# Turning the on-chip memory layout of a one-layer decoder kernel upside down

## The chip, the cores and the metric

The kernel runs on one core of a Trainium2 chip. The metric is device time in microseconds (us) of one execution of the whole program, from a launch to its end; several runs of one program are compared by their median. A profiled execution gives the start and length of every instruction as well.

SBUF is the core's on-chip memory: 128 partitions, each with its own byte addresses. [...] PSUM is the small memory that TensorE (PE) writes its products to. In one matmul the *stationary* operand (here 128x128, brought in by a weight load, PEld) stays in the array, and the *moving* operand (here mostly 128x512) streams through it. VectorE (DVE), ScalarE (ACT) and GpSimd (POOL) do the rest, and SyncE (SP) issues the DMAs.

## The reference

One decoder layer on x of 1024 tokens by 1024 channels, all float32 (cut to what is computed here):

```
def reference(x, ...):
    h = rms_norm(x, norm_mix_g)
    x = x + pool_mixer(h, pool_w, pool_b, pool_scale)   # causal windows 2, 4, 8, 16, then a 256x256 product per group
    f = conv_ffn(rms_norm(x, norm_ffn_g), w_in, conv_w, conv_b, w_out)
    return x + f

def conv_ffn(x, w_in, conv_w, conv_b, w_out):
    h = causal_depthwise_conv(x @ w_in, conv_w, conv_b)   # 1024 -> 2 * 2816, three taps
    val, gate = jnp.split(h, 2, axis=-1)
    return (jax.nn.silu(gate) * val) @ w_out              # 2816 -> 1024
```

## The kernel before

The work has three stages.

**The mixer** (to about 92 us) goes over eight tiles of 128 tokens. Its two products, `psd` (windows, line 152) and `psy` (pool weights, line 206), and the transposing product `pst` (line 229) run on PE. It leaves the second norm's output as operands of the first large product.

**The first product** (x @ w_in) goes over 22 pairs of hidden blocks `n`. Each pair is done as seven half-size products (Strassen-Winograd) instead of eight, the entries `P1` to `P7` of the table `STEPS`:

```
"P1": ("A11", "B11", "X"), "P6": ("S2", "T2", "Y"), "P5": ("S1", "T1", "Z"), "P2": ("A12", "B21", "X"),
"P7": ("S3", "T3", "Y"), "P3": ("S4", "B22", "Z"), "P4": ("A22", "T4", "Y"),
```

The first name is the stationary operand (from the weights), the second the moving one (from the activations), the third the PSUM bank. Every float32 operand is split into a high and a low half, and a step is twelve matmuls of 128x512 (function `product`, line 295): for each of four k, high x high, high x low, low x high. In the profile the moving tiles' numbers are cut off, so that a step is known by its stationary tile: `X<-B,A11s` is P1 (moving B11), `Y<-T,S2s` P6 (T2), `Z<-T,S1s` P5 (T1), `X<-B,A12s` P2 (B21), `Y<-T,S3s` P7 (T3), `Z<-B,S4s` P3 (B22), `Y<-T,A22s` P4 (T4). From n = 2 on the steps run in the order of the table.

**The second product** (gated hidden units @ w_out, line 567) is done in the same way, seven times eleven blocks of twelve matmuls, `oP<-oBP,oAP`. Both operands, moving (`oB..`) and stationary (`oA..`), are split tiles made just before use.

What matters here is where tiles lie. Tiles come from pools. A pool opened plainly is put at the lowest free address, one opened with `side="right"` at the highest:

- `nop_a` (left side): moving tiles B11, T1 and B21 of the first product, 16 KB each, from address 17,312 to 66,464.
- `work` (left side): above it. It holds `raw` (weights as loaded, 76,704 to 93,088) and `hl` (seven split tiles of 4 KB, 93,088 to 121,760). The stationary operands of the first product and both operands of the second are `hl` tiles, made by `split` (lines 69 and 70).
- `n2_pool`, later `late`, later `fin` (left side): above `work`.
- `pre` (right side): all of the mixer's own tiles, from 159,456 up. When the mixer is done, `nop_b` takes its place, with the moving tiles B22, T4, T3 and T2 at 163,808, 180,192, 196,576 and 212,960, and `right` with a small tile.

In the second product, `take` (blocks `blk`) reuses the room of `raw` and of the moving tiles.

Of the kernel before, what the change touches and what calls it, by code (L numbers as in the profile page):

```python
# [14 lines left out]
P = 128  # L15
# [8 lines left out]
WINDOWS = (2, 4, 8, 16)  # L24
HALO = 16
EPS = 1e-6
# Columns of the packed per-partition parameters: conv taps, conv bias, gains of the norms.
CW, CB, GM = 0, 3 * 2 * NF, 4 * 2 * NF
GF = GM + NK
NPAR = GF + NK  # L30
# Columns of the packed constants: identity, factors of the first rows, windows of the first tile.
FAC = P
B0 = FAC + 2 * NG * HALO
BD = B0 + NG * P
# Operands of the first product that are ready before the mixer ends; columns of the second norm's gain that ScalarE applies.
NOPS_A = 3
ACT_GAIN = 7

# [5 lines left out]
def trunk_kernel(ctx: ExitStack, tc: tile.TileContext, x, consts, par, rows, pool_w, w_in, w_out, out):  # L44
# [2 lines left out]
    const = ctx.enter_context(tc.tile_pool(name="const", bufs=1))  # L47
    dram = ctx.enter_context(tc.tile_pool(name="dram", bufs=1, space=bass.MemoryType.DRAM))
    ps_x = ctx.enter_context(tc.tile_pool(name="ps_x", bufs=2, space=PSUM))
    nop_a = ctx.enter_context(tc.tile_pool(name="nop_a", bufs=1))  # L50
    work = ctx.enter_context(tc.tile_pool(name="work", bufs=1))
    mid = ExitStack()
    n2_pool = mid.enter_context(tc.tile_pool(name="n2_pool", bufs=1))
    pre = ExitStack()
    pp = pre.enter_context(tc.tile_pool(name="pre", bufs=1, side="right"))
    ps_p = pre.enter_context(tc.tile_pool(name="ps_p", bufs=3, space=PSUM))

    def bank2(name):
# [2 lines left out]
    def raw_tile(name):  # L61
        return work.tile([P, 2, D], F32, tag="raw", name=name, bufs=2)
# [7 lines left out]
        nc.vector.tensor_tensor(t[:, 1, :], src, t[:, 0, :].bitcast(F32), ALU.subtract)  # L70
        return t

# [1 line left out]
    xs = {}  # L74

    def load_x(j):
# [10 lines left out]
    def affine(t, src, op, fill, base, pattern, step):  # L87
        nc.gpsimd.affine_select(out=t, in_=src, compare_op=op, fill=fill, base=base, pattern=pattern, channel_multiplier=step)

    nc.gpsimd.memset(x_edge[:HALO, :], 0.0)  # L90
    for g, w in enumerate(WINDOWS):
        # Row (j, r) is x[128 j - 16 + r], column (j', t) is token 128 j' + t: 1 / w where j == j' and r - 16 > t - w
        e = edge_band[:, g, :].rearrange("p (j t) -> p j t", t=HALO)
        nc.gpsimd.memset(edge_band[:, g, :], 1.0 / w)
        affine(e, e, ALU.is_gt, 0.0, w - HALO, [[-HALO, NS], [-1, HALO]], 1)
        affine(e, e, ALU.is_ge, 0.0, HALO - 1, [[HALO, NS], [0, HALO]], -1)
    for g, w in enumerate(WINDOWS):
        # 1 / w where s - w < s' <= s, less 1 where s' == s
        m = band[:, g, :]
        nc.gpsimd.memset(m, 1.0 / w)  # L100
        affine(m, m, ALU.is_ge, 0.0, 0, [[1, P]], -1)
        affine(m, m, ALU.is_gt, 0.0, w, [[-1, P]], 1)
        affine(m, m, ALU.not_equal, 1.0 / w - 1.0, 0, [[1, P]], -1)
# [24 lines left out]
    def rstd_of(src, name):  # L128
        junk = pp.tile([P, D], BF16, tag="junk", name=f"junk_{name}")
        st = pp.tile([P, 4], F32, tag="st", name=f"st_{name}", bufs=8)  # L130
        nc.scalar.activation(junk, src, AF.Square, accum_out=st[:, 0:1])
        nc.scalar.activation(st[:, 1:2], st[:, 0:1], AF.Sqrt, bias=eps_t, scale=1.0 / D)
        nc.vector.tensor_scalar(st[:, 0:1], st[:, 0:1], 1.0 / D, EPS, op0=ALU.mult, op1=ALU.add)
        nc.vector.reciprocal(st[:, 2:3], st[:, 1:2])
        # One Newton step on 1 / sqrt
        nc.vector.scalar_tensor_tensor(st[:, 3:4], st[:, 2:3], st[:, 0:1], st[:, 2:3], op0=ALU.mult, op1=ALU.mult)  # L136
        nc.vector.tensor_scalar(st[:, 3:4], st[:, 3:4], -0.5, 1.5, op0=ALU.mult, op1=ALU.add)
        nc.vector.tensor_tensor(st[:, 2:3], st[:, 2:3], st[:, 3:4], ALU.mult)
        return st[:, 2:3]
# [3 lines left out]
    def edge_norm():  # L143
        nc.vector.tensor_scalar(edge_band, edge_band, rstd_of(x_edge, "e"), None, op0=ALU.mult)
# [13 lines left out]
        windows(ps, x_edge, edge_band)  # L158
        nc.scalar.activation(edges, ps.rearrange("p (c s) -> p c s", c=NK), AF.Copy)

# [1 line left out]
    wph = pp.tile([P, 2 * NG, GRP], F32R, tag="wph", name="wph")  # L162
    wpl = pp.tile([P, 2 * NG, GRP], F32R, tag="wpl", name="wpl")

# [32 lines left out]
    def mixer_out(j):  # L197
        dh, dl = ds.pop(j)
        ps = bank2(f"psy{j}")
        for g in range(NG):  # L200
            o = ps[:, g * GRP : (g + 1) * GRP]
            n = 0
            for k in range(2):
                c = 2 * g + k
                for a, w in ((dh, wph), (dh, wpl), (dl, wph)):
                    nc.tensor.matmul(o, a[:, c, :], w[:, c, :], start=n == 0, stop=n == 5)  # L206
                    n += 1
        x1 = xs.pop(j)
        marks[j] = nc.vector.tensor_tensor(x1, ps, x1, ALU.add).ins  # L209
        nc.sync.dma_start(x1_dram[j * P : (j + 1) * P, :], x1)  # L210
        r = rstd_of(x1, f"b{j}")
        diag = pp.tile([P, P], F32, tag="diag", name=f"diag{j}", bufs=2)
        nc.vector.tensor_scalar(diag, ident, r, None, op0=ALU.mult)
        n2s[j] = (x1, diag)
# [36 lines left out]
        nc.scalar.activation(h, src, AF.Copy)  # L251
        nc.vector.tensor_tensor(t[:, 1, ks, cols], src, h.bitcast(F32), ALU.subtract)  # L252

# [1 line left out]
    order = [j + k * NP2 for j in range(NP2) for k in range(2)]  # L255
    raws, sums, aops = {}, {}, {}

# [7 lines left out]
    def add(out, a, b):  # L265
        nc.vector.tensor_tensor(out, a, b, ALU.add)
# [35 lines left out]
    banks, hid = {}, {}  # L302
# [69 lines left out]
        if p == "P4":  # L372
            gated(n)

# [1 line left out]
    def stat(j):  # L376
        if j in xs and j not in stats:
            stats[j] = rstd_of(xs[j], f"a{j}")
# [24 lines left out]
        stat(j + 2)  # L403
        stat(j + 1)
    pre.close()
    nop_b = ctx.enter_context(tc.tile_pool(name="nop_b", bufs=1, side="right"))
    right = ctx.enter_context(tc.tile_pool(name="right", bufs=1, side="right"))
    ps_yz = ctx.enter_context(tc.tile_pool(name="ps_yz", bufs=3, space=PSUM))
    for b in ("T2", "T3", "B22", "T4"):
        nops[b] = nop_tile(nop_b, b)  # L410
# [5 lines left out]
    halves = [slice(0, 2), slice(2, 4)]  # L416
# [16 lines left out]
        split_n(nops["T4"], t4[:, ks], ks=ks)  # L433
    mid.close()
    late_stack = ExitStack()
    late = late_stack.enter_context(tc.tile_pool(name="late", bufs=1))
    for k in range(9, len(events)):
        event(k)
    late_stack.close()

# [1 line left out]
    fin = ctx.enter_context(tc.tile_pool(name="fin", bufs=1))  # L442
    free = []

    def take(name):
        """Room for [P, 512] of float32, where the first product's operands were."""
        if not free:
            take.n += 1
            if take.n <= 2:
                t = raw_tile(f"blk{take.n}").rearrange("p a (b s) -> p (a b) s", s=NH)  # L450
            elif take.n <= 9:
                pool = nop_a if take.n in (3, 5, 6) else nop_b
                t = pool.tile([P, 8, NH], F32, tag="nop", name=f"blk{take.n}", bufs=NOPS_A if pool is nop_a else 7 - NOPS_A)
            else:
                return work.tile([P, NH], F32, tag="q1", name=f"blk_{name}", bufs=2)
            free.extend(t[:, i, :] for i in range(t.shape[1]))
        return free.pop(0)
# [12 lines left out]
    def load_block(name, f):  # L470
        t = blk[name, f] = take(f"{name}_{f}")
        nc.sync.dma_start(t, src[name](f))
# [38 lines left out]
    def z_tile(name, i):  # L511
        return fin.tile([P, NH], F32, tag="z", name=f"{name}_{i}", bufs=12)
# [1 line left out]
    starts = []  # L514

    def z_start(name, i, rows_, cols):
        """x1's block plus the first product."""
        z = zs[name, i] = z_tile(name, i)
        r = rows_ * NH + i * P
        nc.sync.dma_start(z, x1_dram[r : r + P, s_half[cols]])  # L520
        add(z, z, zs["q1", i])
# [15 lines left out]
    for k in range(-SLOOK, len(oevents)):  # L537
# [14 lines left out]
        if f == 0 and opens:  # L552
            for i in range(4):
                tag = ("XXYY" if set_ == "X" else "YZZZ")[i]
                pool = ps_x if tag == "X" else ps_yz
                obanks[set_, i] = pool.tile([P, NH], F32, tag=tag, name=f"o{p}{i}")
        # The last blocks of the last product go bank by bank, so that all banks but one leave early
        if k >= len(oevents) - TAIL:
            if f < NP2 - 1:
                continue  # L560
# [3 lines left out]
        for i, g in steps:  # L564
            a, b = oops[p, g]
            for m, (u, v) in enumerate(((0, 0), (0, 1), (1, 0))):
                nc.tensor.matmul(  # L567
                    obanks[set_, i], a[:, u, i * P : (i + 1) * P], b[:, v, :],
                    start=opens and g == 0 and m == 0, stop=g == NP2 - 1 and m == 2, skip_group_check=not opens,
# [24 lines left out]


def constants():
    """What the windows' shapes alone decide."""
    import numpy as np

    r, t, h = np.arange(P)[:, None], np.arange(P), np.arange(HALO)  # L600
    blocks = [np.eye(P)]
    blocks += [np.tile(w / np.minimum(h + 1, w), (P, 2)) for w in WINDOWS]
    inside = [(r > t - w) & (r <= t) for w in WINDOWS]
    blocks += [(m - np.eye(P) * np.minimum(t + 1, w)) / w for m, w in zip(inside, WINDOWS)]
    return np.concatenate(blocks, axis=1).astype(np.float32)
# [34 lines left out]
```

## Time and profile before

| | before |
|---|---|
| median of 3 runs | 739.74 us |
| the runs | 738.17, 739.74, 740.25 us |
| profiled execution: span from first to last instruction | 736.8 us |
| PE busy in that span | 700.1 us (95%) |
| DVE busy | 627.6 us (85%) |
| ACT busy | 352.3 us (48%) |
| DMA | 83.83 MB |

The page of the profile gives no total time of the profiled execution beside its span. The median of the runs is 2.9 us above the span; that is what lies around the first and the last instruction.

In rows of the timeline the columns are: start in us, length in us, engine, line of the kernel, operation, what it writes `<-` what it reads, shapes and how many instructions were merged into the row. Matmuls are pipelined: the length of one is longer than the distance to the next, so the pace of PE is read from the starts. `PEclk` is the granted TensorE clock as a share of full speed.

### The profile page before, as it was taken

To read this page: it belongs to the slowest core of one execution; us is meant where nothing else is said; L and a number is where in the kernel's file an instruction comes from. 1 tells how busy PE (TensorE), PEld (TensorE's weight loads), DVE (VectorE), ACT (ScalarE), POOL (GpSimd) and SP (SyncE) were. 2 spreads that over 40 slices of the span, in tenths; PEclk is the share of its full clock that TensorE was granted. 3 is DMA by queue.
4 is the path that set the end of the run, shared out by engine and by line. 5 is a ranking of instruction groups with operands and counts; after the bars stand their busy time and mean duration, and the time that the engine had idled before them with its cause. 6 is when DMAs were issued, how large, how long until landed. Compare 5 with 4: busy or idle time off the path is not lost.

```text
span 736.8 us, 8791 instructions
## 1 busy us (share of the span) xinstructions
PE 700.1 (95%) x3236; PEld 579.9 (79%) x3236; DVE 627.6 (85%) x928; ACT 352.3 (48%) x565; POOL 48.0 (7%) x52
## 2 busy tenths in 40 slices
PE   4688869999999999999999999999999999999997
PEld 3688857888888888888888888888887788888886
DVE  3899999999988888888888888877996898698993
ACT  5478654645444444444444444444543344444441
POOL 4523360000000000000000000000000000000000
PEclk9899989999999999999999999999999999999999
DMA  9531103133222222112122222226988920005341
GB/s 280 199 144 57 59 0 115 35 133 119 86 82 67 80 86 81 67 67 80 79 86 86 86 85 87 86 85 210 329 298 291 321 93 1 0 1 171 101 157 57
DMA packets 30882, 83.83 MB, mean 114 GB/s; under 512 B 3335, under 2 KB 4487, under 8 KB 28023
## 3 DMA queue, kind: packets, MB, share of 16 engines
q1 hardware_dynamic: 30839, 83.28, 32.3%
q8 instruction: 25, 0.41, 0.2%
q14 instruction: 18, 0.15, 0.1%
HBM read 63.34 MB, written 19.92 MB: 113 GB/s over the span
## 4 chain that ended last, share of the span: by engine, by line
PE 73%; DVE 14%; DMA 8%; issue 2%; ACT 2%; SPq 1%; DVEq 0%; ACTq 0%
PE Y L295 23%; PE oP L567 21%; PE Z L295 14%; PE X L295 14%; DMA blk<-g_dram 3%; DMA blk<-in_w_out_dram 2%; DMA x<-in_x_dram 1%; DVE T L252 1%; DVE wp_raw L168 1%; PE psy L206 1%; DMA B21s<-in_w_out_dram 1%; DVE x L209 1%; DVE dl L191 1%; DMA A12s<-g_dram 1%; DVE st_b L136 1%
## 5 line engine op out<-in xcount | busy, mean ns | idle before, releaser
L567 PE MATMUL oP<-oBP,oAP 128*128 128x512 f32 x924 | 211.3, 390 | 2.6 <-DVE oBP L70 1.7
L567 PEld LDWEIGHTS oP<-oBP,oAP 128*128 128x128 f32 x924 | 173.1, 188 | 40.6 <-DVE oBP L70 3.1
L295 PE MATMUL Z<-T,S1s 128*128 128x512 f32 x264 | 66.7, 403 | 4.4 <-DVE T L252 3.0
L295 PE MATMUL Z<-B,S4s 128*128 128x512 f32 x264 | 64.1, 392 | 1.5 <-ACT S3s L69 1.5
L295 PE MATMUL Y<-T,S3s 128*128 128x512 f32 x264 | 64.5, 393 | 0.6 <-DVE q L324 0.6
L295 PE MATMUL X<-B,A11s 128*128 128x512 f32 x264 | 64.6, 393 | 0.0
L295 PE MATMUL Y<-T,S2s 128*128 128x512 f32 x264 | 64.3, 392 | 0.0
L295 PEld LDWEIGHTS Z<-T,S1s 128*128 128x128 f32 x264 | 51.0, 194 | 16.9 <-DVE T L252 3.3
L295 PE MATMUL Y<-T,A22s 128*128 128x512 f32 x264 | 64.0, 391 | 0.0
L295 PE MATMUL X<-B,A12s 128*128 128x512 f32 x264 | 63.4, 389 | 0.0
L295 PEld LDWEIGHTS Z<-B,S4s 128*128 128x128 f32 x264 | 49.4, 188 | 12.9 <-ACT S3s L69 1.9
L295 PEld LDWEIGHTS Y<-T,S3s 128*128 128x128 f32 x264 | 49.5, 188 | 12.1 <-DVE q L324 1.0
L295 PEld LDWEIGHTS Y<-T,S2s 128*128 128x128 f32 x264 | 49.6, 188 | 11.2
L295 PEld LDWEIGHTS X<-B,A11s 128*128 128x128 f32 x264 | 49.4, 188 | 11.2
L295 PEld LDWEIGHTS Y<-T,A22s 128*128 128x128 f32 x264 | 49.6, 188 | 10.8
L295 PEld LDWEIGHTS X<-B,A12s 128*128 128x128 f32 x264 | 49.5, 188 | 10.3
L69 ACT ACTIVATE oBP<-blk 128x512 fp32r<-128x512 f32 x32 | 20.2, 633 | 46.9 <-PE oP L567 41.6
L353 ACT ACTIVATE gate<-gate 128x1024 f32<-128x1024 f32 x22 | 23.4, 1062 | 39.6 <-DVE gate L344 39.6
L343 DVE SCALAR_TENSOR_TENSOR val<-ha,par_sb,val 128x1023 f32<-128x1023 f32 x22 | 28.2, 1283 | 12.7 <-ACT val L342 12.7
L335 DVE TENSOR_TENSOR ha<-Z,q 128x512 f32<-128x512 f32 x20 | 13.8, 691 | 24.7 <-PE Z L295 24.7
L342 ACT ACTIVATE gate<-hb,par_sb 128x1024 f32<-128x1024 f32 x22 | 27.4, 1246 | 14.5 <-DVE hb L337 14.4
L342 ACT ACTIVATE val<-ha,par_sb 128x1024 f32<-128x1024 f32 x22 | 27.4, 1244 | 13.4 <-DVE ha L335 4.2
(128 smaller groups left out, 1130.2 us busy)
## 6 DMA issues: line engine op xcount, KB each, us to landing
win<-in_w_in_dram SPq DMA_DIRECT2D x22, 1024.0 KB, 4.8
g_dram<-val SPq DMA_DIRECT2D x22, 512.0 KB, 2.6
blk<-g_dram SPq DMA_DIRECT2D x33, 256.0 KB, 5.4
blk<-in_w_out_dram SPq DMA_DIRECT2D x31, 256.0 KB, 5.5
A12s<-g_dram SPq DMA_DIRECT2D x22, 256.0 KB, 4.5
B21s<-in_w_out_dram SPq DMA_DIRECT2D x22, 256.0 KB, 3.4
x<-in_x_dram SPq DMA_DIRECT2D x8, 512.0 KB, 10.5
x_dram<-x SPq DMA_DIRECT2D x8, 512.0 KB, 2.8
```

What stands on the lines that cost most here:

```text
L69: nc.scalar.activation(t[:, 0, :], src, AF.Copy)
L136: nc.vector.scalar_tensor_tensor(st[:, 3:4], st[:, 2:3], st[:, 0:1], st[:, 2:3], op0=ALU.mult, op1=ALU.mult)
L168: nc.vector.scalar_tensor_tensor(wp_raw[:, c, :], scale_b[:, g * GRP : (g + 1) * GRP], par_sb[:, GM + c : GM + c + 1], wp_raw[:, c, :], op ...
L191: nc.vector.tensor_tensor(dl, ps3, dh.bitcast(F32), ALU.subtract)
L206: nc.tensor.matmul(o, a[:, c, :], w[:, c, :], start=n == 0, stop=n == 5)
L209: marks[j] = nc.vector.tensor_tensor(x1, ps, x1, ALU.add).ins
L295: nc.tensor.matmul(bank, a[:, i, ks], b[:, l, k, :], start=opens and m == 0, stop=m == 11, skip_group_check=not opens)
L335: tt(hid[n, "a"][:, NH:], bank, hid[n, "q2"], ALU.add)
L342: nc.scalar.activation(t, src, AF.Identity, bias=par_sb[:, CB + f : CB + f + 1], scale=w[2])
L343: nc.vector.scalar_tensor_tensor(t[:, 1:], src[:, : S - 1], w[1], t[:, 1:], op0=ALU.mult, op1=ALU.add)
L353: nc.scalar.activation(gate, gate, AF.Silu)
L567: nc.tensor.matmul(obanks[set_, i], a[:, u, i * P : (i + 1) * P], b[:, v, :], start=opens and g == 0 and m == 0, stop=g == NP2 - 1 and m = ...
```

## The change

Pools are opened on the opposite side. `work`, `n2_pool`, `late` and `fin` go to the right side (the top), and `pre`, `nop_b` and `right` to the left (the bottom). `const` and `nop_a` stay. Comments and docstrings are dropped, and one blank line is added near the top, so that the lines of the kernel after stand one further down (295 becomes 296).

```diff
     nop_a = ctx.enter_context(tc.tile_pool(name="nop_a", bufs=1))
-    work = ctx.enter_context(tc.tile_pool(name="work", bufs=1))
+    work = ctx.enter_context(tc.tile_pool(name="work", bufs=1, side="right"))
     mid = ExitStack()
-    n2_pool = mid.enter_context(tc.tile_pool(name="n2_pool", bufs=1))
+    n2_pool = mid.enter_context(tc.tile_pool(name="n2_pool", bufs=1, side="right"))
     pre = ExitStack()
-    pp = pre.enter_context(tc.tile_pool(name="pre", bufs=1, side="right"))
+    pp = pre.enter_context(tc.tile_pool(name="pre", bufs=1))
...
-    nop_b = ctx.enter_context(tc.tile_pool(name="nop_b", bufs=1, side="right"))
-    right = ctx.enter_context(tc.tile_pool(name="right", bufs=1, side="right"))
+    nop_b = ctx.enter_context(tc.tile_pool(name="nop_b", bufs=1))
+    right = ctx.enter_context(tc.tile_pool(name="right", bufs=1))
...
-    late = late_stack.enter_context(tc.tile_pool(name="late", bufs=1))
+    late = late_stack.enter_context(tc.tile_pool(name="late", bufs=1, side="right"))
...
-    fin = ctx.enter_context(tc.tile_pool(name="fin", bufs=1))
+    fin = ctx.enter_context(tc.tile_pool(name="fin", bufs=1, side="right"))
```

The two built programs have the same instructions in the same order on every engine and the same semaphore waits with the same values. They differ in the SBUF addresses of tiles alone:

| tiles | address before | address after |
|---|---|---|
| moving, first product: B11, T1, B21 | 17,312 to 66,464 | the same |
| moving, first product: B22, T4, T3, T2 | 163,808 to 229,344 | 66,464 to 132,000 |
| `hl`: stationary of the first product, both operands of the second | 93,088 to 121,760 | 196,576 to 225,248 |
| `raw`: weights as loaded | 76,704 to 93,088 | 180,192 to 196,576 |
| the mixer's pool weights `wph`, `wpl` (moving) and `dh`, `dl` (stationary) | 193,248 to 209,632 and 216,032 to 228,320 | 100,256 to 116,640 and 123,040 to 135,328 |

## The prediction

> **What bounds the kernel now.** I read the page first: busy times, the clock, and the chain of work that ended last.
>
> ```profile
> span 736.8 us, 8791 instructions
> PE 700.1 (95%) x3236; PEld 579.9 (79%) x3236; DVE 627.6 (85%) x928; ACT 352.3 (48%) x565; POOL 48.0 (7%) x52
> PEclk9899989999999999999999999999999999999999
> PE 73%; DVE 14%; DMA 8%; issue 2%; ACT 2%; SPq 1%; DVEq 0%; ACTq 0%
> ```
>
> PE is busy 95% of the span and carries 73% of the chain, and after the mixer its clock is full: whatever changes the pace of a matmul changes the time. Busy time by stretch (us of the stretch, then busy us and instructions of PE, PEld, DVE, ACT and POOL, clock, DMA share, GB/s) says where:
>
> ```profile
> 119.00:519.00 400.00, 399.44 (x1741) 326.47 (x1740) 341.94 (x442) 187.57 (x252) 0.00 (x0) 1.00 0.25 92
> 525.00:737.00 212.00, 205.35 (x899) 168.02 (x897) 177.63 (x287) 87.78 (x150) 0.00 (x0) 1.00 0.43 141
> 306.95:326.23 19.28, 19.28 (x85) 15.77 (x84) 16.28 (x22) 8.96 (x12) 0.00 (x0) 1.00 0.23 82
> ```
>
> From 119 to 519 us, the first product, PE hardly stops (0.56 us in 400), while DVE has 58 us to spare. The third row is one pair n: PE without a gap, DVE 16.28 of 19.28 us. The second product waits 6.65 us in 212.
>
> The change moves no instruction and no wait; it moves addresses. So the question is whether an address shows in the pace of anything. The timeline of PE for that pair n, one row a step of twelve matmuls:
>
> ```profile
> 306.95 2.93 PE L295 MATMUL X<-B,A11s 128*128 128x512 f32 x12
> 309.72 2.93 PE L295 MATMUL Y<-T,S2s 128*128 128x512 f32 x12
> 312.48 2.93 PE L295 MATMUL Z<-T,S1s 128*128 128x512 f32 x12
> 315.25 2.88 PE L295 MATMUL X<-B,A12s 128*128 128x512 f32 x12
> 317.97 2.93 PE L295 MATMUL Y<-T,S3s 128*128 128x512 f32 x12
> 320.74 2.91 PE L295 MATMUL Z<-B,S4s 128*128 128x512 f32 x12
> 323.48 2.91 PE L295 MATMUL Y<-T,A22s 128*128 128x512 f32 x12
> 326.23 2.93 PE L295 MATMUL X<-B,A11s 128*128 128x512 f32 x12
> ```
>
> The distance from one start to the next is the cost of a step: P1 2.77, P6 2.76, P5 2.77, P2 2.72, P7 2.77, P3 2.74, P4 2.75 us, in all 19.28. Equal work, no gap, full clock, and yet nearly 2% between them. It is not the bank: P1 and P2 both write X. It isn't what runs beside them either, since the same figures come back at the first pairs, where DVE and ACT do other work:
>
> ```profile
> 138.96 2.93 PE L295 MATMUL Z<-T,S1s 128*128 128x512 f32 x12
> 141.73 2.88 PE L295 MATMUL X<-B,A12s 128*128 128x512 f32 x12
> 144.45 2.93 PE L295 MATMUL Y<-T,S3s 128*128 128x512 f32 x12
> 147.22 2.91 PE L295 MATMUL Z<-B,S4s 128*128 128x512 f32 x12
> 149.96 2.91 PE L295 MATMUL Y<-T,A22s 128*128 128x512 f32 x12
> 152.71 2.93 PE L295 MATMUL X<-B,A11s 128*128 128x512 f32 x12
> ```
>
> (2.77, 2.72, 2.77, 2.74, 2.75 again.) It fits with where the moving tile lies. P3, P4, P6 and P7 stream from `nop_b`, above 163,808, with the stationary tiles at 93,088 to 121,760: slow, 2.74 or 2.75 in the steps that follow another such step, 2.76 or 2.77 in those that come after a step from `nop_a`. P2, P1 and P5 stream from `nop_a`, below 66,464. P2, which follows another of its kind (P5), is the fast one, 2.72. P1 and P5 follow slow ones and pay 0.05 for the way back, as if two streams had to fall into step again. The spread inside the groups agrees (operation, count, then minimum, median and maximum ns):
>
> ```profile
> L295 PE MATMUL X<-B,A11s x264: 387/393/473, 74.6 to 502.3; 128*128 128x512 f32 x132
> L295 PE MATMUL X<-B,A12s x264: 387/389/476, 90.7 to 510.5; 128*128 128x512 f32 x132
> L295 PE MATMUL Z<-B,S4s x264: 388/392/503, 110.4 to 516.1; 128*128 128x512 f32 x132
> L295 PE MATMUL Y<-T,A22s x264: 388/392/394, 125.2 to 518.8; 128*128 128x512 f32 x132
> ```
>
> **What is known of other pairs of places.**
>
> ```profile
> 599.71 25.55 PE L567 MATMUL oP<-oBP,oAP 128*128 128x512 f32 x112
> 77.47 0.28 PE L206 MATMUL psy<-wph,dh 128*128 128x256 f32 x1
> 80.22 0.28 PE L206 MATMUL psy<-wph,dl 128*128 128x256 f32 x1
> ```
>
> Second product, both operands in `hl`: 112 matmuls in 25.55 us, the last of them 0.39 long as in the group's mean, so (25.55 - 0.39) / 111 = 0.2267 us each, 2.72 for twelve: the fast form. Mixer, both operands at the top (`wph` from 193,248, `dh` and `dl` from 216,032), columns 256: 24 matmuls whose first and last starts are 2.75 apart, 0.1196 each and even. So an operand high up is not slow by itself; the pair decides.
>
> **The parts of the change.**
>
> *First product.* After it all seven moving tiles lie at 17,312 to 132,000 and all stationary ones at 196,576 to 225,248. No row shows a moving tile far below its stationary one by that much; the nearest is P2 (moving at 50,080, stationary at 93,088): 2.72. All the slow rows have the moving tile above. By the sign alone all seven steps become like P2, and the two returns fall away as well: 7 x 2.72 = 19.04 against 19.28, -0.24 a pair. Pairs of the clean order run from 152.71 to 521 us, 19 of them: -4.6. Of the steps ahead of them, the five shown from 138.96 to 152.71 take 13.75 against 5 x 2.72 = 13.60, 0.15 over; the seven or so from 119 us on, at the same rate, 0.2. Together -0.4; sum -5.0. The other end for the same unknown: all seven stay at the dearest step, 2.77, or 19.39 a pair: 19 x 0.11 = 2.1, and 12 early steps x 0.02 = 0.2: +2.3. In between lies the steady slow form (2.74 and 2.75, 19.22): -0.06 x 19 = -1.1. I take -5.0, the value of the nearest row by order of the two places.
>
> *Second product.* Both operands move together from 93,088 to 196,576; their distances to each other stay. The nearest rows are itself and `psy`, both even and fast: 0. If the height of the moving tile did count for 512 columns, 77 times twelve matmuls go from 2.72 to 2.75: +2.3.
>
> *Mixer.* `psy` moves as a whole from top to bottom; 0. Its PE has gaps anyway.
>
> *DVE and ACT.* Blocks `blk` lie in `nop_b`, `nop_a` and `raw`, so at both ends, some of them 64 bytes off:
>
> ```profile
> L70 DVE TENSOR_TENSOR oAP<-blk,oAP x44: 674/683/694, 504.0 to 723.2; 128x512 fp32r<-128x512 f32 x44
> L69 ACT ACTIVATE oAP<-blk x44: 614/616/635, 503.2 to 722.4; 128x512 fp32r<-128x512 f32 x44
> ```
>
> At most 20 ns of spread in 44 places: no address price, 0. They also have slack (DVE 16.28 of what would be 19.04), so PE's gain isn't taken back by them.
>
> *DMA and what is late next.* The loads of the second product wait for the first product's moving tiles to be free, and between 513 and 560 us the chain runs over them:
>
> ```profile
> 513.56 5.52 DMA blk<-in_w_out_dram
> 530.35 6.17 DMA blk<-in_w_out_dram
> 699.84 33.11 PE oP L567 x145
> ```
>
> They start when the last steps end, so they start earlier by as much; the gain passes through. From 699.84 to the end the chain is PE's own. Same tiles and sizes: 0.
>
> **Sum.** -5.0 us on the profiled span: 736.8 to 731.8. The median lies 2.9 above the span (739.74), so 734.7. What a measurement of this kernel can tell from no change is about 0.3%, 2.2 us.
>
> **Rivals.**
>
> *A. The offset decides, not the order.* Another reading fits all the rows above as well. Distance from moving to stationary start: `nop_a` to `hl` 75,776 = 148 x 512, nothing left over; `hl` to `hl` multiples of 4,096; `wph` to `dh` 22,784, a multiple of 256. Only `nop_b` to `hl`, 70,720 = 138 x 512 + 64, is off, by 64 bytes. The right side ends where its tiles end, not on the left side's grid. After the change `hl` sits on the right side's grid and every moving tile on the left's: 179,264 = 350 x 512 + 64. Then all seven steps are in the steady slow form, without returns: -1.1, or 738.6. For it: two streams that must fall into step after each switch look like a clash by low address bits. Against it: the 64 bytes now lie on the other side.
>
> *B. The height of the moving tile decides.* First product -5.0, second +2.3: -2.7, 737.0. Against it: `psy`'s even 0.1196.
>
> *C. Slower: the search for step never ends.* If the order low under high is the worse one, what P1 and P5 pay on their way back (2.77) becomes every step's price: +2.3, 742.0. It turns slower once the mean step is above 19.28 / 7 = 2.754. For it: 2.77 is paid just by low moving tiles, with nothing left to account for. Against it: P2 settles.
>
> *D. Nothing.* 739.7, if what separates P2 from the rest is its place in the order and not its tile. Against it: P5, after P6, moves like P1, after P4, and at 138.96 to 152.71 the neighbours are others.
>
> [...]
>
> **Chances.** Forecast 0.42, A 0.33, B 0.08, C 0.12, D 0.05. The forecast's own range is 733.5 to 736. The range over the cases reaches from a full gain to D with the runs' spread, and leaves out most of C: 733.2 to 741. Faster by over 0.3%: the forecast and half of B, 0.46; within 0.3%: A, D, half of B, 0.42; slower: C, 0.12.
>
> **What would show it.** Right: in PE's timeline all seven steps 2.72 apart and a pair 19.04; medians of 389 ns in every group; the second product still 0.2267. A: all steps 2.74 or 2.75, P2 too. B: second product at 2.75 for twelve. C: steps of 2.77 and P2 among them. The forecast is wrong if P2's row, which doesn't move itself, gets slower when its stationary tile does.

## The result, and the profile after

The kernel after takes 744.9 us (median of 6 runs, 743.9 to 747.41), the kernel before 739.2 us in the same comparison (6 runs, 737.96 to 740.25): ratio 1.0094, 95% interval 1.0077 to 1.0112. It is slower by 0.9%. Forecast were 734.7 us and a range from 733.2 to 741.0.

The page after, the lines that answer to those of before:

```profile
span 743.2 us, 8791 instructions
PE 707.3 (95%) x3236; PEld 580.7 (78%) x3236; DVE 628.6 (85%) x928; ACT 352.3 (47%) x565; POOL 48.0 (6%) x52
PEclk9899989999999999999999999999999999999999
PE 80%; DVE 11%; DMA 4%; ACT 2%; issue 2%; SPq 0%; DVEq 0%; ACTq 0%
```

The long stretch of the first product by busy time (columns as in the prediction):

```profile
119.00:519.00 400.00, 399.55 (x1713) 321.61 (x1712) 340.24 (x437) 185.53 (x250) 0.00 (x0) 1.00 0.23 86
```

The same instructions, the same granted clock (1.00 from 119 to 519 us), PE 7.2 us longer busy, weight load (PEld), DVE and ACT within 1 us of before. In the 400 us of the last row PE is as full as before, but has 1713 matmuls where it had 1741. So each takes longer. The timeline of PE for one pair n:

```profile
310.85 2.96 PE L296 MATMUL X<-B,A11s 128*128 128x512 f32 x12
313.65 2.96 PE L296 MATMUL Y<-T,S2s 128*128 128x512 f32 x12
316.45 2.96 PE L296 MATMUL Z<-T,S1s 128*128 128x512 f32 x12
319.25 2.96 PE L296 MATMUL X<-B,A12s 128*128 128x512 f32 x12
322.05 2.96 PE L296 MATMUL Y<-T,S3s 128*128 128x512 f32 x12
324.85 2.96 PE L296 MATMUL Z<-B,S4s 128*128 128x512 f32 x12
327.65 2.96 PE L296 MATMUL Y<-T,A22s 128*128 128x512 f32 x12
330.45 2.96 PE L296 MATMUL X<-B,A11s 128*128 128x512 f32 x12
```

Every step starts 2.80 us after the one before: a pair is 19.60 against 19.28. No step differs from the next, and P2 (`X<-B,A12s`), whose moving tile B21 did not move, went from 2.72 to 2.80. Nineteen such pairs cost 19 x 0.32 = 6.1 us. The first product ends 7.4 us later (526.45 against 519.03): besides those 6.1, its first matmul already starts 0.8 later (75.39 against 74.62), and the steps ahead of the nineteen pairs add 0.6. The second product, from its first matmul's start to its last's, takes 1.1 us less (212.4 against 213.5), because it waits less between its steps (1.6 us idle before its matmuls against 2.6); so the span grows by 6.4 (all rounded). Weight load and matmul of P1 and P2 side by side (minimum, median and maximum ns):

```profile
L296 PEld LDWEIGHTS X<-B,A11s x264: 187/188/192, 75.4 to 509.2; 128*128 128x128 f32 x132
L296 PE MATMUL X<-B,A11s x264: 392/397/482, 75.4 to 509.4; 128*128 128x512 f32 x132
L296 PE MATMUL X<-B,A12s x264: 393/398/478, 91.4 to 517.8; 128*128 128x512 f32 x132
```

The matmul of P2 was 389 and is 398; a weight load is 188 ns. The second product kept its pace:

```profile
593.81 36.43 PE L568 MATMUL oP<-oBP,oAP 128*128 128x512 f32 x160
```

(36.43 - 0.39) / 159 = 0.2267 us each, as before.

### The profile page after: what moved, and what is told of

It reads as the page before. It is cut to its first block, busy times and chain, and to the rows that moved or that the text cites. A ratio compares the mean times of both kernels' runs of the same rounds, so it can differ in the third digit from the quotient of the medians.

```text
span 743.2 us, 8791 instructions
## 1 busy us (share of the span) xinstructions
PE 707.3 (95%) x3236; PEld 580.7 (78%) x3236; DVE 628.6 (85%) x928; ACT 352.3 (47%) x565; POOL 48.0 (6%) x52
## 4 chain that ended last, share of the span: by engine, by line
PE 80%; DVE 11%; DMA 4%; ACT 2%; issue 2%; SPq 0%; DVEq 0%; ACTq 0%
PE Y L296 24%; PE oP L568 24%; PE Z L296 15%; PE X L296 15%; DMA x<-in_x_dram 1%; DMA B21s<-in_w_out_dram 1%; DVE T L253 1%; DVE wp_raw L169 1%; PE psy L207 1%; DMA blk<-g_dram 1%; DVE x L210 1%; DVE dl L192 1%; DVE st_b L137 1%; DMA A12s<-g_dram 1%; DVE st_a L139 1%
## 5 line engine op out<-in xcount | busy, mean ns | idle before, releaser
L296 PE MATMUL X<-B,A12s 128*128 128x512 f32 x264 | 65.1, 396 | 0.0
L322 ACT ACTIVATE ha<-X 128x512 f32<-128x512 f32 x22 | 13.1, 596 | 44.3 <-PE X L296 40.7
```

The source lines that it names most:

```text
L296: nc.tensor.matmul(bank, a[:, i, ks], b[:, l, k, :], start=opens and m == 0, stop=m == 11, skip_group_check=not opens)
L322: nc.scalar.activation(hid[n, "a"][:, :NH], bank, AF.Copy)
```

## The experiments

Two theories were set against each other. **L**: what counts is the distance from the start of the stationary tile up to that of the moving one, by its low bits (rival A of the prediction, and a possible sign). **O**: what counts is which of the two lies higher, or at which end (the forecast and rival C). The kernel after, in these terms: distance from stationary up to moving, in bytes within a partition, 17,312 - 196,576 = -179,264 = -351 x 512 + 448. "Remainder" below is what such a distance leaves by 512, here 448. The remainders follow from the addresses in the built programs.

**e1, 64 unused bytes at the top** (of the kernel after, in place of the added blank line; the instructions keep their order):

```diff
+    pad = ctx.enter_context(tc.tile_pool(name="pad", bufs=1, side="right")).tile([P, 16], F32, tag="pad", name="pad")
     nop_a = ctx.enter_context(tc.tile_pool(name="nop_a", bufs=1))
     work = ctx.enter_context(tc.tile_pool(name="work", bufs=1, side="right"))
```

> The kernel after with 64 unused bytes at the very top, so that everything on the right side lies 64 bytes lower and the distance from every moving tile of the first product to the hl tiles is a multiple of 512. Theory L (the low bits of the distance between moving and stationary start decide): all seven steps of a pair take 2.72 us, P2 too, a pair 19.04; against 2.80 after, that is 7 x 0.08 x 22 = 12.3 us off, about 733 us, and some 5 us under the kernel before. Theory O (the order of the two places decides, low under high is slow): nothing changes, 2.80 a step, 744.9.

Measured 733.06 us against 738.45 for the kernel before, ratio 0.9936 (0.9912 to 0.996). PE's timeline:

```profile
312.73 2.88 PE L296 MATMUL X<-B,A12s 128*128 128x512 f32 x12
315.45 2.88 PE L296 MATMUL Y<-T,S3s 128*128 128x512 f32 x12
318.17 2.88 PE L296 MATMUL Z<-B,S4s 128*128 128x512 f32 x12
320.89 2.88 PE L296 MATMUL Y<-T,A22s 128*128 128x512 f32 x12
```

2.72 a step, all of them. Sixty-four idle bytes are worth 0.08 us a step, with the moving tiles still low and the stationary ones high. O falls, and with it the sense in which I had read the profile.

**e2, the same 64 bytes at the top of the kernel before.** Its moving tiles B22, T4, T3 and T2 stay high, 64 bytes lower.

```diff
-    nop_a = ctx.enter_context(tc.tile_pool(name="nop_a", bufs=1))
+    nop_a = ctx.enter_context(tc.tile_pool(name="nop_a", bufs=1));pad = ctx.enter_context(tc.tile_pool(name="pad", bufs=1, side="right")).tile([P, 16], F32, tag="pad", name="pad")
     work = ctx.enter_context(tc.tile_pool(name="work", bufs=1))
```

> The kernel before with 64 unused bytes at the very top, so that the right side's moving tiles (B22, T4, T3, T2) lie 64 bytes lower, a multiple of 512 from the hl tiles; they stay above the stationary tiles. Theory L: all seven steps 2.72, a pair 19.04 instead of 19.28, -5 us, about 734.5. Theory O: steps as before, 2.74 to 2.77, time as before.

Measured 733.94 us, ratio 0.9939 (0.9917 to 0.9961):

```profile
311.81 2.88 PE L295 MATMUL Z<-T,S1s 128*128 128x512 f32 x12
314.53 2.88 PE L295 MATMUL X<-B,A12s 128*128 128x512 f32 x12
317.25 2.88 PE L295 MATMUL Y<-T,S3s 128*128 128x512 f32 x12
```

2.72 again, without turning anything round. e1 and e2 are both 0.6% faster than the kernel before, and their intervals overlap.

**e3, 64 bytes low in the kernel before**, between the low moving tiles and `hl` (the edit of e2 without `side="right"`):

> The kernel before with 64 unused bytes between the low moving tiles and the work pool: hl lies 64 bytes higher, so that B11, T1 and B21 stand 64 bytes short of a multiple of 512 from it and the four tiles at the top stand right. Theory L: the roles are swapped: P3 and P4 come down to 2.72, P2 rises to 2.80 (as after), P1 and P5 near 2.80, returns at P6 and P7. Theory O: steps as before, P2 2.72, P3 2.74, P4 2.75.

Measured: 738.18 us (one run).

```profile
308.51 2.96 PE L295 MATMUL X<-B,A11s 128*128 128x512 f32 x12
311.31 2.90 PE L295 MATMUL Y<-T,S2s 128*128 128x512 f32 x12
314.05 2.96 PE L295 MATMUL Z<-T,S1s 128*128 128x512 f32 x12
316.85 2.96 PE L295 MATMUL X<-B,A12s 128*128 128x512 f32 x12
319.65 2.90 PE L295 MATMUL Y<-T,S3s 128*128 128x512 f32 x12
322.39 2.88 PE L295 MATMUL Z<-B,S4s 128*128 128x512 f32 x12
325.11 2.88 PE L295 MATMUL Y<-T,A22s 128*128 128x512 f32 x12
327.83 2.96 PE L295 MATMUL X<-B,A11s 128*128 128x512 f32 x12
```

The roles are swapped as L says: P1, P5 and P2 with the low tiles 2.80 (remainder 448, as in the kernel after), P3 and P4 with the high ones 2.72, and P6 and P7, which come after a slow step, 2.74. The high place was never the matter.

**e4, 128 bytes at the top of the kernel after**: remainder 64, the one that the high tiles had before.

> The kernel after with 128 unused bytes at the top: moving tiles still below the stationary ones, but now 64 bytes past a multiple of 512 instead of 64 short of it. Theory L with a sign: the steady slow form of before, 2.74 or 2.75 for all seven steps, a pair 19.22. L without a sign (modulus of 128): 2.80 as after. Theory O: 2.80 as after.

Measured: 736.94 us (one run).

```profile
308.15 2.91 PE L296 MATMUL X<-B,A11s 128*128 128x512 f32 x12
310.90 2.91 PE L296 MATMUL Y<-T,S2s 128*128 128x512 f32 x12
313.65 2.91 PE L296 MATMUL Z<-T,S1s 128*128 128x512 f32 x12
316.39 2.91 PE L296 MATMUL X<-B,A12s 128*128 128x512 f32 x12
```

2.75, 2.75, 2.74: exactly the steady form of before, though the order of the two places is the opposite. So 64 past a multiple costs 0.027 a step and 64 short of it 0.08. This is the kernel that rival A had in mind.

**e5 to e8, other paddings at the top of the kernel after** (192, 320, 448 and 96 bytes in place of 64):

> As the 64-byte pad, with 192 unused bytes: moving start minus stationary start leaves 128 by 512. Theory L1 (the pattern repeats every 128 bytes or less, with a sign inside): 2.72 a step. Theory L2 (it repeats every 256): neither 2.72 nor known; half a turn away, so something between 2.72 and 2.80 or more. Theory L3 (every 512): likewise unknown. Anything but 2.72 excludes L1.

> 320 unused bytes: remainder 256. L1 and L2: 2.72 a step, about 733. L3: not 2.72. The mixer's psy product, even at a remainder of 256 with 256 columns, speaks for 2.72.

> 448 unused bytes: remainder 384. L1: 2.72. L2: the same as with remainder 128. L3: another value than with 128 and 256.

> 96 unused bytes: remainder 32. If the price grows from 0 at 0 bytes to 0.027 us a step at 64, it is about 2.73 here; if places are told apart only by blocks of 64 bytes, it is 2.72 or 2.747; more than 2.75 means that the price doesn't grow with distance at all.

Measured: 746.04, 733.31, 742.76 and 746.51 us (one run each). Two starts of each, in that order:

```profile
310.36 2.96 PE L296 MATMUL X<-B,A11s 128*128 128x512 f32 x12
313.16 2.96 PE L296 MATMUL Y<-T,S2s 128*128 128x512 f32 x12
```

```profile
310.99 2.88 PE L296 MATMUL Z<-T,S1s 128*128 128x512 f32 x12
313.71 2.88 PE L296 MATMUL X<-B,A12s 128*128 128x512 f32 x12
```

```profile
309.25 2.95 PE L296 MATMUL X<-B,A11s 128*128 128x512 f32 x12
312.04 2.95 PE L296 MATMUL Y<-T,S2s 128*128 128x512 f32 x12
```

```profile
312.30 2.96 PE L296 MATMUL X<-B,A11s 128*128 128x512 f32 x12
315.10 2.96 PE L296 MATMUL Y<-T,S2s 128*128 128x512 f32 x12
```

Remainder 128 costs 2.80, so the pattern does not repeat every 128 bytes (L1 falls). Remainder 256 is free, 2.72. Remainder 384 gives 2.78 to 2.80 from step to step. Remainder 32 costs 2.80, more than 64 does: the price doesn't grow with distance, and the first two cases of the expectation, 2.73 and 2.72 or 2.747, are out.

**e9, 64 bytes at the bottom of the kernel after**, so that the moving tiles move and the stationary ones don't (the line of e1 without `side="right"`):

> The kernel after with 64 unused bytes at the bottom, ahead of the moving tiles, and nothing at the top: now the moving tiles move up by 64 and the stationary ones stay where the kernel after has them. Theory L (only the distance counts): 2.72 a step as with the 64 bytes at the top, about 733. If the absolute place of the stationary tiles in the grid counted, it stays at 2.80, about 745.

Measured: 734.69 us (one run).

```profile
311.45 2.88 PE L296 MATMUL Z<-T,S1s 128*128 128x512 f32 x12
314.17 2.88 PE L296 MATMUL X<-B,A12s 128*128 128x512 f32 x12
```

The step is 2.72: it is the same whichever of the two tiles is shifted.

**e10, `hl` tiles 4,160 bytes apart** instead of 4,096, on e1. Now neighbouring `hl` tiles, the operands of the second product, are off each other's grid too, and within a pair of the first product each step has a remainder of its own: P1 128, P6 192, P5 384, P2 448, P7 320, P3 256 and P4 64.

```diff
-        return work.tile([P, 2, NH], F32R, tag="hl", name=name, bufs=7)
+        return work.tile([P, 2 * NH + 16], F32R, tag="hl", name=name, bufs=7)[:, : 2 * NH].rearrange("p (a s) -> p a s", a=2)
...
-            xs[j] = work.tile([P, D], F32, tag="hl", name=f"x{j}", bufs=7)
+            xs[j] = work.tile([P, D + 16], F32, tag="hl", name=f"x{j}", bufs=7)[:, :D]
```

> The kernel with the 64-byte pad at the top, and each of the seven hl tiles 64 bytes longer than it needs (4,160 apart): the two operands of the second product, which lie in neighbouring places, now stand off the grid of 256 bytes from each other. Theory L: the second product, at 2.72 for twelve matmuls in every kernel so far, slows down to 2.75 to 2.80 on the mean, 77 x 0.03 to 0.08 = 2 to 6 us; the steps of the first product have a remainder of their own each (P3 256, the others not a multiple of 256), a pair takes 19.2 to 19.6. If the effect belongs to the first product's tiles or places alone, the second product stays at 2.72.

Measured: 744.04 us (one run). One pair of the first product, then a stretch of the second, then the second product's group (busy us, mean ns):

```profile
304.10 2.89 PE L296 MATMUL Z<-B,S4s 128*128 128x512 f32 x12
306.83 2.92 PE L296 MATMUL Y<-T,A22s 128*128 128x512 f32 x12
309.58 2.96 PE L296 MATMUL X<-B,A11s 128*128 128x512 f32 x12
312.38 2.96 PE L296 MATMUL Y<-T,S2s 128*128 128x512 f32 x12
315.18 2.96 PE L296 MATMUL Z<-T,S1s 128*128 128x512 f32 x12
317.97 2.96 PE L296 MATMUL X<-B,A12s 128*128 128x512 f32 x12
320.77 2.91 PE L296 MATMUL Y<-T,S3s 128*128 128x512 f32 x12
323.52 2.89 PE L296 MATMUL Z<-B,S4s 128*128 128x512 f32 x12
...
599.63 30.62 PE L568 MATMUL oP<-oBP,oAP 128*128 128x512 f32 x131
```

```profile
L568 PE MATMUL oP<-oBP,oAP 128*128 128x512 f32 x924 | 215.0, 394 | 0.2 <-DVE oBP L71 0.2
```

(30.62 - 0.39) / 130 = 0.2325 us a matmul, 2.79 for twelve in this stretch, and 215.0 us busy in the whole, where the kernel before has 211.3: the second product, at remainder 0 in every other layout, slows down with the others. A pair of the first takes 19.42, and its steps order themselves by their remainders: P3 (256) takes 2.73, P4 (64) and P7 (320, which is 256 + 64) 2.75, the other four 2.79 or 2.80. So the pattern repeats every 256 bytes, as far as these values go. This also speaks against an effect of what DVE and ACT write meanwhile: all moving tiles lie on one grid of 512 bytes here, and the steps of one pair still differ, 2.73 to 2.80, each by its own stationary tile.

**e11, 512 bytes at the top of the kernel after**:

> 512 unused bytes at the top: the remainder by 512 is again that of the kernel after (448). If the pattern repeats every 512 bytes or less, all steps take 2.80, matmuls alternate between 231 and 236 ns as there, about 745; if it doesn't, something else.

Measured: 744.36 us (one run); starts 2.80 apart as in the kernel after.

```profile
310.55 2.96 PE L296 MATMUL X<-B,A11s 128*128 128x512 f32 x12
313.35 2.96 PE L296 MATMUL Y<-T,S2s 128*128 128x512 f32 x12
```

The runs together, us for a step of twelve matmuls of 128x512, by the distance from stationary to moving start (steady form; in e10 each step follows one with another remainder):

| remainder by 512 | step | where |
|---|---|---|
| 0 | 2.72 | P2 before, e1, e2, P3 and P4 in e3, e9, second product |
| 32 | 2.80 | e8 |
| 64 | 2.747 | P3 and P4 before, e4 (P4 in e10: 2.75) |
| 128 | 2.80 | e5, P1 in e10 |
| 192 | 2.80 | P6 in e10 |
| 256 | 2.72 | e6 (P3 in e10: 2.73) |
| 320 | 2.75 | P7 in e10 |
| 384 | 2.78 to 2.80 | e7, P5 in e10 |
| 448 | 2.80 | after, P2 in e3, P2 in e10, e11 |

## Why the prediction was wrong

**What held.** PE's pace in the first product is the bound (PE busy 399.55 of 400 us after), the clock is full there (1.00), and what the pace gains or loses passes through to the end: e1 changes a pair from 19.60 to 19.04, 22 x 0.56 = 12.3 us, and the span of the profiled execution falls by 12.1, from 743.2 to 731.1 (the medians, 744.9 and 733.06, come from two comparisons). The pace depends on where the two operands lie; the reading of 2.72, 2.75 and 2.77 as a fast form, a slow form and the way back was right (e3 shows the three kinds again, 2.72, 2.80 and 2.74, with the tiles exchanged). DVE and ACT at 0 held: the rows of `blk` are alike before and after (means: DVE 683 and 681 ns, ACT 618 and 618). The second product stayed at 0.2267, which disposes of rival B. Mixer and second product were not at 0 to the tenth, 0.8 later and 1.1 shorter, but that is not the change's doing as far as the runs show: in e1, turned round as well, the first product's first matmul starts at 74.5 us, and over all the runs the second product's matmuls and the idle time before them take 211.5 to 214.5 us (e10 left out).

**Small readings.** The prediction adds 2.9 us from the span to the median, as what lies around the first and the last instruction. In every run whose span is on record the time is only 1.7 or 1.8 us above it, so an execution with a span of 736.8 takes about 738.5, and the rest was spread between runs. With 1.7 the forecast would have been 733.5, no nearer. ACT's row of `blk` spreads by 21 ns (614 to 635), not by 20 at most, and PE's part of the chain from 699.84 on ends at 732.94, with a DVE addition after it. None of this bears on the outcome.

**The step that failed** is "By the sign alone all seven steps become like P2": the choice of the value by the order of the two places. All seven took 2.80 in place of 2.72, a pair 19.60 in place of 19.04, so that the -4.6 of the nineteen pairs came out as +6.1. Two readings fitted every row, order and 64-byte offset, and I gave the forecast to the order, because P2 was the nearest row by place. It was the farthest by what counts: P2's distance is a multiple of 512, and after the change no step's is. e1 and e2 settle it with 64 bytes each.

**Rival A** had the quantity and not its size. It put 179,264 = 350 x 512 + 64 beside 70,720 = 138 x 512 + 64 as if they were alike; but one goes up and the other down from the stationary tile, and 64 short is not 64 past. Its own objection, that the 64 bytes now lie on the other side, was the point: 2.80 where it had 2.74 or 2.75. With 2.80 its sum is 19 x (19.60 - 19.28) = +6.1 in place of -1.1; measured are +6.4 on the span and +5.7 on the median.

**Rival C** got the sign with the wrong cause. Its price, 2.77, was taken as the dearest that a step can cost, since it was the dearest row. That row was a mean over twelve matmuls whose pace changed within the step: in P1 at 306.95 the first ten start 225 to 236 ns apart, and the last ones 226 and 227, the spacing of P2. The steady form after, 230 to 236 ns throughout, is dearer, 2.80, and so the range ended at 741.0, below the result.

**Rival D** fell with the same rows: P2 has the same place in the order of steps in every kernel, and takes 2.72 before, 2.80 after and in e3, 2.72 in e1.

**The check that was at hand.** The prediction ends with "The forecast is wrong if P2's row, which doesn't move itself, gets slower when its stationary tile does", and that is what happened.

**What stays open.** The runs show that the distance between the moving and the stationary operand decides (2.80 after, 2.72 in e1 and e9, which move one operand each by 64 bytes), and that the matmul gets longer (389 to 398 ns) while the weight load stays at 188. They don't show by what means the distance acts, why 64 is cheaper than 32, 128 and 448, or whether other widths than 512 columns pay as much. Whether 128 and 384, 2.80 and 2.78 to 2.80, are the same is not settled either: at 128 the steps of e5 and P1 of e10 take 2.80, and at 384 those of e7 vary from 2.78 to 2.80 and P5 of e10 takes 2.79, less than the others by 0.02 at most.

## What to carry to other kernels

When equal matmul steps at full clock differ by one or two per cent, compare the addresses of their two operands: here a distance that is a multiple of 256 bytes gave 0.2267 us per 128x512 matmul in the steady form, any other tried 0.229 to 0.233. A pool that is opened from the other side, or a small tile ahead of it, can shift that distance without a trace in the instructions; 64 idle bytes bought 0.6% here (e1 and e2). And where two readings fit all rows of a profile, name the number in which they differ, and don't bound an unknown form by the dearest row that happened to occur.

## What the runs showed of the hardware that was not expected

- At a granted clock of 1.00 (119 to 519 us, before, after and in e1), the pace of the float32 128x512 matmuls, each with a weight load, went with what the distance between their operands' addresses leaves by 512: 226.7 ns at 0 (e1) and 256 (e6), 228.9 ns at 64 (e4), 233.3 ns at 32 (e8), 128 (e5) and 448 (after) (steps of 2.72, 2.747 and 2.80 divided by twelve).
- The price has a sign: 64 bytes past a multiple of 512 cost 2.2 ns a matmul (e4), 64 short of it 6.7 ns (the kernel after).
- A step at remainder 0 that followed one with another remainder took longer: 2.77 for its twelve matmuls in the kernel before where the steady form is 2.72, and 2.74 in e3, coming from 2.80.
- Where in SBUF the tiles lie, at the top or the bottom, above or below each other, made no difference to the step once the remainder was 0: 2.72 in e1, e2 and e9.
